# A hybrid decoder layer: the first quarter's input scale computed on TensorE, and the second quarter's embedding moved behind the first head

## The chip, the core and the metric

The kernel runs on one core of a Trainium2 chip. A core has five engines that work side by side, each through its own list of instructions in order: TensorE (PE, matrix products), VectorE (DVE), ScalarE (ACT), GpSimd (POOL) and SyncE (SP), which here only issues transfers. Transfers (DMA) run on the core's 16 DMA engines between device memory and the on-chip buffers. Matrix products accumulate in PSUM, which this kernel uses as eight banks of 128 x 512 fp32 values.

The metric is the device time of one execution in microseconds (us). The median of three runs of the kernel before is 2885.75 us, the lowest 2883.01 and the highest 2885.87.

## The reference, cut to what matters

One decoder layer over T = 2048 tokens with D = 1024 channels, all in fp32. Beside x there is an input p with 256 channels per token.

```python
hn   = rms_norm(x, pre_mix_norm)          # x * rsqrt(mean(x*x) + 1e-6) * w, per token
proj = hn @ w_in                          # q, k, v, z of 4 delta-rule heads; f, i, q, g of 4 HGRN heads; a, b
o_a  = gated delta rule on silu(conv(q, k, v)), decays from a, b, in chunks   # a triangular solve per chunk
o_b  = HGRN2 recurrence from f, i, q
h    = x + rms_norm(concat(o_a * silu(z), o_b * silu(g)) @ w_out, post_mix_norm)
y    = square(relu(rms_norm(h, pre_mlp_norm) @ w_mlp_up)) @ w_mlp_down
h    = h + rms_norm(y, post_mlp_norm)
e    = rms_norm(p @ w_ple_proj, ple_norm) # the embedding: 256 -> 1024 channels
out  = h + e * sigmoid(h @ w_ple_gate)
```

Two results matter here. The scale of x, one rsqrt(mean(x*x) + eps) for each token, is needed before any in-projection can start. The embedding e = p @ w_ple_proj with the sum of its squares is needed only at the very end of the layer.

## The kernel before

**Tiling.** Tokens are worked in four quarters of 512 (`QT`). Activations lie transposed: 128 channels on the partitions, 512 tokens along the row, so that x of a quarter is eight tiles of 128 x 512. Each fp32 operand is split in two float32r halves (`split`, L159 to L162): ACT writes the rounded value (L161), DVE the remainder (L162). A product of two operands is three matmuls (high by high, high by low, low by high), 128 x 128 by 128 x 512 each. A weight of the in-projection is 1024 x 128: it is loaded to a `raw` buffer (two of them, 512 KB), split into a `whl` buffer (three of them), and takes part in 24 matmuls.

**The front** (L329 to L374). PE computes the embedding of quarters 0 and 1, eight tiles each, six matmuls a tile (`embed_tile`, L292, `project`, L190). ACT copies each tile to a buffer `e` (six of them) for a store to device memory (`ed`), and squares it; DVE adds the squares (`squares`, L217). The embedding weight comes in two loads of four tiles (`stage_ple`, L277). For the scale, 2 MB of x are loaded by rows, tokens on the partitions (L338); ACT squares each 1024-wide row with an accumulated sum (L355), POOL raises the four sums per partition to the power -0.5 (`rsqrt`, L156). The result, 128 x 4, is written to device memory (`spread`, L228) and read back as a row that is broadcast to all partitions (`spread_load`, L234). Between the later embedding tiles each of the eight transposed tiles of x is scaled by it and by the norm's weight (`operand`, L197, the scaling L203) and split: these are the in-projection's operands `xt`. `vectors` (L130 to L146) makes the small per-channel constants from the transposed vectors.

**The mixers** (L377 to L935). `works` (L792 to L802) lists the in-projections in order: for each quarter the decays' `ab`, then for each of four heads eight projections (k, q, v, z of the delta rule, f, i, q, g of HGRN). Each is 24 matmuls, done in three steps of eight; after each step `tick()` (L324) runs the parts of other generators that the agenda has at that step. So the written program places, by step number: the delta-rule mixer (`gdn_mixer`, with offsets `A_STEPS` from the head's first projection), the HGRN mixer (`B_STEPS`), the decays (`decays`, L427, ending in the transposes `ps_gb`, L450), the norms of the embedding (`norm_steps`, L255: a split of the sum, two matmuls with ones, a row by way of device memory), the next quarter's scale (`x_scale`, L399, from step 30 of the quarter) and its operands (`load_x`, L820), and the sums of MLP weights (`down_sums`, L859). In quarter 0 `stage_work` loads the weight three works ahead, `split_work` splits it two works ahead, and `keep_work` stores the split weight, which later quarters reload.

**The first head's solve.** `gdn_mixer` sends the four diagonal blocks of its triangular systems through device memory (`ud`, L582 to L589), solves them on DVE in 31 dependent pairs of multiply and reduce (L595, L596, four rows to a step), stores the result (`xd`, L600), loads it back as diagonal blocks (`xx`, L606), transposes (L610), and goes on with the matmuls `psp` (L618).

**What sets the order.** PE's order is the written one throughout (`manual_schedule`, L301). SP's order, and so the order of DMA issues, is written in the front and in the mixers' loop (L331, L889). The orders of DVE, ACT and POOL are chosen by a planner that sorts the instructions of the whole program. Buffers of a pool (`bufs`) make a writer wait for the last reader of the same buffer.

## Time and profile before

| what | value |
|---|---|
| runs, median (lowest to highest) | 2885.75 us (2883.01 to 2885.87) |
| profiled execution, its own time | 2882.39 us |
| span of the profiled execution | 2880.6 us |
| mean granted TensorE clock | 0.988 of full speed |
| PE busy, share of the span | 2780.4 us, 97% |
| DVE busy | 2155.5 us, 75% |
| ACT busy | 1332.7 us, 46% |
| POOL busy | 132.8 us, 5% |
| moved by DMA | 589.71 MB, 205 GB/s in the mean |

The span is that of the instructions; the execution's own time includes what lies around them, 1.8 us here. Rows of the trace that follow give, in order of time: start in us from the span's start, duration in us, engine, line of the kernel, instruction, output and inputs by the program's names, shapes, and how many were grouped ("x24": from the first start to the last end). In brackets stands how long the engine had waited before it and what released it. SPq is SP's queue issuing a DMA. In the page's groups, "A <- B: 12.3, 1, 12.3" is a wait of PE for B ahead of A: sum, count, mean. In the table of stretches each row is one stretch: its bounds, its length, then busy time and number of instructions of PE, weight loads (PEld), DVE, ACT and POOL, then the granted clock of TensorE, the busy share of the DMA engines, and GB/s.

### The profile page before, as it was taken

How to read it: one execution, taken by the hardware profiler on the slowest of the kernel's cores; microseconds unless marked ns; L12 is line 12 of the kernel's file. 1: busy time of each engine (PE TensorE's matmuls, PEld its weight loads, DVE VectorE, ACT ScalarE, POOL GpSimd, SP SyncE). 2: the span in 40 equal slices, each digit the busy share in tenths (PEclk: the TensorE clock that was granted, in tenths of full speed). 3: DMA queues.
4: the chain of work that ended last, by engine and by line, in shares of the span. 5: the costliest groups of instructions: out<-in, count | busy, mean ns of one | idle time of the engine just before them, and what ended most of it. 6: DMA issues, size and time to landing. Idle time of an engine off the chain costs nothing.

```text
span 2880.6 us, 39562 instructions
## 1 busy us (share of the span) xinstructions
PE 2780.4 (97%) x13361; PEld 2296.8 (80%) x13361; DVE 2155.5 (75%) x4700; ACT 1332.7 (46%) x2460; POOL 132.8 (5%) x116
## 2 busy tenths in 40 slices
PE   7899999999999999889999999999999999999999
PEld 5688788888888888767778887888888888887887
DVE  6788788887878787747879987776787765567675
ACT  6444333333324333447556555554555445465431
POOL 0000000000000000120000000000100000001000
PEclk9899999999999999999999999999999999999999
DMA  7666667656655666577746646666664446677563
GB/s 253 228 215 204 221 208 245 204 189 222 220 192 177 209 201 201 177 240 236 250 134 217 235 161 221 221 209 196 210 202 146 157 150 210 188 257 240 194 230 118
DMA packets 268603, 589.71 MB, mean 205 GB/s; under 512 B 55642, under 2 KB 59960, under 8 KB 249072
## 3 DMA queue, kind: packets, MB, share of 16 engines
q1 hardware_dynamic: 268400, 587.18, 61.2%
q8 instruction: 106, 1.74, 0.3%
...
## 4 chain that ended last, share of the span: by engine, by line
PE 47%; DMA 4%; DVE 4%; ACT 2%; issue 2%; POOL 1%; SPq 1%; DVEq 0%; ACTq 0%; POOLq 0%
PE u L953 21%; PE d L953 18%; PE mmg L953 6%; DMA mixT<-mixd 1%; PE mmo L953 1%; DMA da<-sumd 1%; DMA rsb_g<-rd_g 0%; DMA b<-h1d 0%; DMA xo<-in_xT_dram 0%; DMA raw_out<-in_w_out_dram 0%; PE mme L188 0%; DMA dr<-in_w_down_dram 0%; POOL acc_y L225 0%; DVE w_out L162 0%; POOL w_out L162 0%
## 5 line engine op out<-in xcount | busy, mean ns | idle before, releaser
L907 PE MATMUL mm<-xt,w 128*128 128x512 f32 x3072 | 791.5, 405 | 1.0 <-ACT hist L478 1.0
L907 PEld LDWEIGHTS mm<-xt,w 128*128 128x128 f32 x3072 | 564.8, 191 | 120.7 <-ACT hist L478 1.7
L953 PE MATMUL u<-t,wu 128*128 128x512 f32 x2688 | 627.3, 395 | 6.3 <-ACT wu L161 5.2
L953 PE MATMUL d<-db,da 128*128 128x512 f32 x2688 | 612.8, 390 | 4.0 <-ACT db L214 2.0
L953 PEld LDWEIGHTS u<-t,wu 128*128 128x128 f32 x2688 | 507.0, 189 | 125.8 <-ACT wu L161 6.7
L953 PEld LDWEIGHTS d<-db,da 128*128 128x128 f32 x2688 | 504.1, 188 | 112.0 <-DVE db L215 4.4
L215 DVE TENSOR_TENSOR db<-db 128x512 fp32r<-128x512 f32 x224 | 160.6, 717 | 76.0 <-ACT db L214 75.4
L1273 DVE TENSOR_TENSOR u<-u,u 128x512 f32<-128x512 f32 x224 | 150.4, 683 | 68.5 <-PE u L953 68.5
L953 PE MATMUL mmo<-mixT,w_out 128*128 128x512 f32 x768 | 186.7, 404 | 13.4 <-DVE w_out L162 6.3
L953 PEld LDWEIGHTS mmo<-mixT,w_out 128*128 128x128 f32 x768 | 148.2, 194 | 50.7 <-DVE w_out L162 8.0
L214 ACT ACTIVATE db<-db 128x512 fp32r<-128x512 f32 x224 | 140.9, 629 | 87.5 <-DMA db<-hid 82.9
L953 PE MATMUL mmg<-h2T,wg 128*128 128x512 f32 x768 | 177.5, 393 | 0.0
L953 PEld LDWEIGHTS mmg<-h2T,wg 128*128 128x128 f32 x768 | 144.3, 188 | 32.8
L595 DVE TENSOR_TENSOR pr_g<-xs_g,sys_g 128x4 f32<-128x4 f32 (+30 forms) x496 | 138.7, 280 | 32.9 <-DMA sys_g<-ud_g 22.8
L1313 ACT ACTIVATE u<-u 128x512 f32<-128x512 f32 x128 | 80.9, 632 | 170.5 <-DVE u L1273 170.2
L162 DVE TENSOR_TENSOR da<-da 128x512 fp32r<-128x512 f32 x128 | 93.8, 733 | 85.8 <-ACT da L161 85.2
L161 ACT ACTIVATE da<-da 128x512 fp32r<-128x512 f32 x128 | 80.5, 629 | 130.6 <-DMA da<-sumd 114.1
L596 DVE TENSOR_REDUCE xs_g<-pr_g 128x4 f32<-128x8 f32 (+30 forms) x496 | 111.0, 224 | 9.9
L161 ACT ACTIVATE wu<-a 128x512 fp32r<-128x512 f32 x128 | 76.4, 622 | 56.4 <-DMA a<-in_w_up_dram 54.4
L225 POOL TENSOR_TENSOR acc_y<-acc_y,sq_y 128x512 f32<-128x512 f32 x28 | 38.6, 1379 | 1379.1 <-ACT sq_y L224 1379.1
L162 DVE TENSOR_TENSOR wu<-a,wu 128x512 fp32r<-128x512 f32 x128 | 87.5, 687 | 8.5 <-ACT wu L161 8.2
L706 PE MATMUL at_h<-q_h,k_h 128*128 128x64 f32 x640 | 82.7, 273 | 2.1 <-DVE tail_g L528 1.4
(355 smaller groups left out, 3839.9 us busy)
## 6 DMA issues: line engine op xcount, KB each, us to landing
...
db<-hid SPq DMA_DIRECT2D x224, 256.0 KB
...
a<-in_w_up_dram SPq DMA_DIRECT2D x128, 256.0 KB
hid<-u SPq DMA_DIRECT2D x128, 256.0 KB
da<-sumd SPq DMA_DIRECT2D x128, 256.0 KB
...
```

What stands on the lines that cost most here:

```text
L161: S.activation(t[:, 0], raw, AF.Copy)
L162: eng.tensor_tensor(t[:, 1], raw, t[:, 0], ALU.subtract)
L214: S.activation(t[:, 0], plain(t), AF.Copy)
L215: V.tensor_tensor(t[:, 1], plain(t), t[:, 0], ALU.subtract)
L225: eng.tensor_tensor(acc, acc, sq, ALU.add)
L595: V.tensor_tensor(pr[:, :, 0:i], xs[:, :, 0:i], sys[:, None, 0:i, i].broadcast_to([P, GC, i]), ALU.mult)
L596: V.tensor_reduce(xs[:, :, i], pr[:, :, 0 : i + 1], AX.X, ALU.add)
L706: PE.matmul(ps[:, c, :], k[:, blk(c)], odd, start=True, stop=True)
L907: PE.matmul(ps, *terms[i], start=i == 0, stop=i == nt - 1)
L953: PE.matmul(ps, a, b, start=start, stop=stop)
L1273: V.tensor_tensor(c[new], c[old], ps, ALU.add)
L1313: S.activation(c[k], c[k], AF.Relu)
```

## The change

1. *The scale of the first x.* The loads of x by rows are gone. The eight transposed tiles of x, loaded anyway, are squared by ACT, two at a time (four operations of 128 x 1024), and added by DVE to one 128 x 512 tile. Four matmuls with one column of ones sum it over the partitions, with 128 tokens on the partitions of each column. After scaling, POOL's power gives the 128 x 4 values; DVE multiplies the identity by them (`diag`), and one fp32 matmul of ones by `diag` gives the scale of every token on all partitions, in a PSUM bank that DVE reads directly when it scales the tiles.
2. *The front's order.* SP, ACT and DVE follow the written order there (`first`), not the planner's. The embedding's eight tiles of quarter 0 go to banks of two pools (`homes`); their squares are kept in four pairs (`esq`) and summed after the operands. `vectors` is split in two: the transposed columns early, the rest after the operands. The weights of `ab` and of the first projection (`4_0_0`) are staged in the front.
3. *The second quarter's embedding* leaves the front. It becomes two works (`plee0`, `plee1`) of 24 matmuls each behind the first head's eight projections of quarter 0, four tiles a work. Its input p is loaded and split from step 16 (`load_p`); each tile is copied to one of two buffers of the pool `m2` and its store is issued at once (`leave`).
4. *What follows from it.* Quarters start at the steps in `qstart`. The second quarter's `x_scale` starts at step 40 rather than 30. The norm of the first embedding runs at steps 2 to 7, that of the second after `plee1`.

The diff, cut to its core (`stage` is moved out of the mixers with its text unchanged; `leave` is the second half of `embed_tile`):

```diff
-    def vectors():
-
+    def columns_of_rows():
         ps = bank("ps_rows", pp)
         PE.transpose(ps[:, :N_ROWS], rows, ident[:N_ROWS, :N_ROWS])
         V.tensor_copy(cols, ps[:, :N_ROWS])
+
+    def vectors():
...
-        def ready(eng):
+        def ready(eng, then=None):
             w = wp.tile([P, 2, KD, P], F32R, tag="whl", name=f"w_{name}")
             for half in range(2):
                 sl = slice(half * KD // 2, (half + 1) * KD // 2)
                 split(w[:, :, sl], eng, raw[:, sl])
+                if half == 0 and then is not None:
+                    then()
+            return w
+
+        return ready
+
+    def stage(name, src, k=KD):
...
+        return leave(ps, q, d, accs, pool, bufs)
+
+    def leave(ps, q, d, accs, pool, bufs):
...
-        with tc.manual_schedule(engines={mybir.EngineType.SP}):
+        first = {mybir.EngineType.SP, mybir.EngineType.Activation, mybir.EngineType.DVE}
+        with tc.manual_schedule(engines=first):
             ple0 = stage_ple(0, "plea0")
-            praw = [es.tile([P, 2, QT], F32, name=f"praw{q}") for q in range(2)]
-            nc.sync.dma_start(praw[0], pT[:, tok(0)].rearrange("(k p) t -> p k t", p=P))
-            rows4 = x[tok(0), :].rearrange("(p c) d -> p c d", c=NC)
-            xs = es.tile([P, NC, D], F32, name="xs")
-            for c in range(0, NC, 2):
-                nc.sync.dma_start(xs[:, c : c + 2], rows4[:, c : c + 2])
+            praw = es.tile([P, 2, QT], F32, name="praw0")
+            nc.sync.dma_start(praw, pT[:, tok(0)].rearrange("(k p) t -> p k t", p=P))
             nc.sync.dma_start(ident, consts[:, C_IDENT])
             nc.sync.dma_start(rows, vecs)
-            nc.sync.dma_start(dec[:, 0:1], gdn_a_log.rearrange("o h -> h o"))
-            nc.sync.dma_start(dec[:, 1:2], gdn_dt_bias.rearrange("o h -> h o"))
-            nc.sync.dma_start(praw[1], pT[:, tok(1)].rearrange("(k p) t -> p k t", p=P))
-            ple1 = stage_ple(1, "plea1")
             xraw = es.tile([P, KD, QT], F32, name="xraw")
             for k in range(0, KD, 2):
                 nc.sync.dma_start(xraw[:, k : k + 2],
                                   xT[k * P : (k + 2) * P, tok(0)].rearrange("(k p) t -> p k t", p=P))
+            nc.sync.dma_start(dec[:, 0:1], gdn_a_log.rearrange("o h -> h o"))
+            nc.sync.dma_start(dec[:, 1:2], gdn_dt_bias.rearrange("o h -> h o"))
+            ple1 = stage_ple(1, "plea1")
+            ab_ready, w0_ready = stage("ab0", w_ab), stage("4_0_0", w_in[4])
             nc.sync.dma_start(cst[:, C_NEG:], consts[:, C_NEG:])
 
-            ple = [ple0(V), None]
-            pts = [[operand(ra, None, f"pT{q}_{k}", raw=praw[q][:, k]) for k in range(2)] for q in range(1)]
+            pt, ple, es_sq, stores = [], {}, {}, []
+            ple[0] = ple0(V, lambda: pt.extend(operand(ra, None, f"pT0_{k}", raw=praw[:, k]) for k in range(2)))
+            p1 = [ra.tile([P, 2, QT], F32R, tag="ring", name=f"pT1_{k}") for k in range(2)]
+            homes = (pm, pm, pp, pp, pp, pp, pm, pm)
+            sums = {}
+
+            def embed(d):
+                sums[d] = bank(f"mme_0_{d}", homes[d])
+                project(sums[d], ple[d // 4][:, :, 2 * (d % 4) : 2 * (d % 4) + 2], pt)
+
+            def put(d):
+                if d % 2 == 0:
+                    es_sq[d // 2] = es.tile([P, 2, QT], F32, name=f"esq{d // 2}")
+                e = es.tile([P, QT], F32, tag="ld", name=f"e0_{d}", bufs=KD)
+                S.activation(e, sums[d], AF.Copy)
+                S.activation(es_sq[d // 2][:, d % 2], sums.pop(d), AF.Square)
+                nc.sync.dma_start(ed[0][d], e)
+
+            total = es.tile([P, 2, QT], F32, name="xtotal")
+
+            def x_squares(k):
+                if k == 0:
+                    S.activation(total, xraw[:, :2], AF.Square)
+                else:
+                    sq = es.tile([P, 2, QT], F32, tag="xsq", name=f"xsq{k}", bufs=2)
+                    S.activation(sq, xraw[:, k : k + 2], AF.Square)
+                    V.tensor_tensor(total, total, sq, ALU.add)
+
+            embed(0)
+            columns_of_rows()
+            x_squares(0)
+            embed(1)
+            put(0)
+            x_squares(2)
+            embed(2)
+            x_squares(4)
+            put(1)
+            embed(3)
+            x_squares(6)
+            acc = st.tile([P, QT], F32, tag="acc", name="acc_x0", bufs=3)
+            V.tensor_tensor(acc, total[:, 0], total[:, 1], ALU.add)
+
+            ps = bank("ss_x0", po)
+            for c in range(NC):
+                PE.matmul(ps[:, c : c + 1], acc[:, blk(c)], one[:, 0:1], start=True, stop=True)
+            ple[1] = ple1(V)
             ss = sm.tile([P, NC], F32, tag="ss", name="ss_x0")
-            for c in range(NC):
-                S.activation(xs[:, c], xs[:, c], AF.Square, accum_out=ss[:, c : c + 1])
-            V.tensor_scalar(ss, ss, 1.0 / D, EPS, ALU.mult, ALU.add)
+            V.tensor_scalar(ss, ps[:, :NC], 1.0 / D, EPS, ALU.mult, ALU.add)
             rsqrt(ss)
-            stores = []
-            for d in range(4):
-                stores.append(embed_tile(0, d, ple[0], pts[0], accs, es, 6))
-                if d == 1:
-                    vectors()
-            pts.append([operand(ra, None, f"pT1_{k}", raw=praw[1][:, k]) for k in range(2)])
-            ple[1] = ple1(V)
-            x_r[0] = spread(ss, "x0")
-            rsb = spread_load(x_r[0], "x0")
-            for d, q in [(d, 1) for d in range(4)] + [(d, q) for d in range(4, KD) for q in range(2)]:
-                stores.append(embed_tile(q, d, ple[d // 4], pts[q], accs, es, 6))
-                stores.pop(0)()
-                if len(xts[0]) < KD:
-                    k = len(xts[0])
-                    xts[0].append(operand(ra, None, f"xt0_{k}", col(R_PREMIX + k), rsb, raw=xraw[:, k]))
-            for f in stores:
-                f()
+            put(2)
+            split_w = {0: ab_ready()}
+            diag = es.tile([P, NC, P], F32, name="xdiag")
+            V.tensor_tensor(diag, over_chunks(ident), ss[:, :, None].broadcast_to([P, NC, P]), ALU.mult)
+            rsb = bank("rs_x0", po)
+            PE.matmul(rsb, one, diag.rearrange("p c n -> p (c n)"), start=True, stop=True)
+            put(3)
+            for d in range(4, KD):
+                embed(d)
+            for k in range(KD):
+                xts[0].append(operand(ra, None, f"xt0_{k}", col(R_PREMIX + k), rsb, raw=xraw[:, k]))
+                if k % 2:
+                    put(4 + k // 2)
+            vectors()
+            pair = es_sq[0]
+            for i in range(1, KD // 2):
+                V.tensor_tensor(pair, pair, es_sq[i], ALU.add)
+            accs[0] = st.tile([P, QT], F32, tag="acc", name="acc_e0", bufs=3)
+            V.tensor_tensor(accs[0], pair[:, 0], pair[:, 1], ALU.add)
...
+        qstart = []
         for q in range(NQ):
+            qstart.append(SPT * len(works))
             works.append((f"ab{q}", "ab", w_ab, q, None, None, None, None))
...
+                if (q, h) == (0, 0):
+                    works += [(f"plee{i}", None, i, 0, None, None, None, None) for i in range(2)]
         last = t + LAST
-        staged, split_w = {}, {}
+        staged = {1: w0_ready}
 
...
-                staged[j] = stage(works[j][0], works[j][2])
+                name, key, src = works[j][:3]
+                staged[j] = stage(name, src) if key else partial(stage_ple(src, name), V)
...
-            if works[j][3] == 0:
+            if works[j][3] == 0 and works[j][1]:
                 keep(works[j][1], split_w[j])
+
+        def load_p():
+
+            raws = [m2.tile([P, QT], F32, tag="ld", name=f"raw_pT1_{k}", bufs=2) for k in range(2)]
+            for k in range(2):
+                nc.sync.dma_start(raws[k], pT[blk(k), tok(1)])
+            yield
+            for k in range(2):
+                split(p1[k], V, raws[k])
 
...
-        per_q = SPT * (1 + 8 * 4)
-        starts = [per_q * q + 5 + n * i for q, m, n in ((1, 6, 14), (2, 5, 16), (3, 5, 16)) for i in range(m)]
+        starts = [qstart[q] + 5 + n * i for q, m, n in ((1, 6, 14), (2, 5, 16), (3, 5, 16)) for i in range(m)]
         for g, t in enumerate(starts):
             at(t, down_sums(g), (0, 4, 6, 10))
         for q in range(1, NQ):
-            at(per_q * (q - 1) + 30, x_scale(q), range(0, 20, 2))
-            at(per_q * q, load_x(q), range(-9, 0))
-            call(per_q * q, boundary)
-        for q in range(2):
-            at(0, norm_steps(accs[q], 1.0 / D, EPS, f"e{q}", partial(ple_r.__setitem__, q)),
-               [4 * q + i for i in (0, 2, 4, 5)])
+            at(qstart[q - 1] + (40 if q == 1 else 30), x_scale(q), range(0, 20, 2))
+            at(qstart[q], load_x(q), range(-9, 0))
+            call(qstart[q], boundary)
+        at(0, norm_steps(accs[0], 1.0 / D, EPS, "e0", partial(ple_r.__setitem__, 0)), (2, 4, 6, 7))
+        at(16, load_p(), (0, 3))
         with tc.manual_schedule(engines={mybir.EngineType.SP}):
-            stage_work(0)
-            stage_work(1)
-            split_work(0)
             stage_work(2)
             split_work(1)
             for j, (name, key, src, q, h, then, g, b) in enumerate(works):
                 split_work(j + 2)
                 stage_work(j + 3)
                 keep_work(j)
+                if key is None:
+                    w = split_w.pop(j)
+                    for s in range(SPT):
+                        for i in range(s * 24 // SPT, (s + 1) * 24 // SPT):
+                            k, term = i % 6 // 3, i % 3
+                            if i % 6 == 0:
+                                ps = bank(f"mme_1_{4 * src + i // 6}")
+                            PE.matmul(ps, w[:, term // 2, 2 * (i // 6) + k, :], p1[k][:, term % 2, :],
+                                      start=i % 6 == 0, stop=i % 6 == 5)
+                            if i % 6 == 5:
+                                leave(ps, 1, 4 * src + i // 6, accs, m2, 2)()
+                        tick()
+                    if src == 1:
+                        at(clock[0], norm_steps(accs[1], 1.0 / D, EPS, "e1", partial(ple_r.__setitem__, 1)),
+                           (1, 3, 5, 6))
+                    continue
                 ps = bank(f"mm_{name}")
                 w, xt = split_w.pop(j), xts[q]
                 terms = []
```

15 lines of the change are left out of this document (6 added, 9 removed).

## The prediction

> **What bounds the kernel now.** I read the page's engine shares first, then a table of stretches of the first 140 us, then what TensorE (PE) waited for there, then its instructions in order of time.
>
> ```profile
> PE 2780.4 (97%) x13361; PEld 2296.8 (80%) x13361; DVE 2155.5 (75%) x4700; ACT 1332.7 (46%) x2460; POOL 132.8 (5%) x116
> ...
> 20.00:30.00 10.00, 4.43 (x19) 3.04 (x17) 5.04 (x8) 5.62 (x10) 0.00 (x0) 0.95 0.96 338
> 120.00:140.00 20.00, 8.72 (x34) 7.66 (x35) 10.73 (x31) 4.41 (x12) 0.00 (x0) 0.57 0.51 171
> ...
> PE psp_g L618 <- DVE xx_g L610: 12.3, 1, 12.3
> ```
>
> PE is busy for 97% of the span, so time is won or lost only where PE stands. In the first 140 us it does so in two places: the front, before the first in-projection matmul (20 to 30 us: 4.43 of 10 busy), and once in the first head, 12.3 us ahead of `psp`, the matmuls that wait for VectorE's (DVE's) triangular solve of that head.
>
> ```profile
> 46.47 5.87 PE L907 MATMUL mm_ab<-xt,w_ab 128*128 128x512 f32 x24 [0.30 <-ACT sq_e L224]
> 52.18 0.40 PE L261 MATMUL nrm_e<-hl_e,ones 128*128 128x512 f32 x1
> ...
> 61.35 1.19 PE L450 MATMUL ps_gb<-cst,gb 36*128 36x36 f32 x4 [0.61 <-DVE gb L442]
> ...
> 83.18 18.91 PE L907 MATMUL mm<-xt,w 128*128 128x512 f32 x80
> ...
> 131.28 2.04 PE L618 MATMUL psp_g<-xx_g,um 128*128 128x128 f32 x8 [12.29 <-DVE xx_g L610]
> ...
> 134.68 3.72 PE L907 MATMUL mm<-xt,w 128*128 128x512 f32 x8
> 138.23 0.60 PE L486 MATMUL t_kg<-cst,y_kg 128*128 128x128 f32 x4
> ...
> 146.94 1.05 PE L618 MATMUL psp_g<-xx_g,um 128*128 128x128 f32 x8
> ```
>
> The reader is to see three marks: in-projection from 46.47, decay transposes `ps_gb` at 61.35, `psp` at 131.28. A warm matmul of 512 columns costs 18.91/80 = 0.236 us. After the stall PE is slow: the 6.95 us from 131.28 to 138.23 hold 8 `psp` (2.04 here, 1.05 at 146.94), 8 `at_h` of like length and 8 matmuls (3.72 here, 1.9 at 0.236 each); at full pace, with their overlaps, that is about 3.7, so the cold restart costs 3.3.
>
> **How the change is to be counted.** Up to `psp` PE passes as many matmuls after the change as before: 34 steps of 8. Before, all 272 belong to the in-projection; after, 48 of them are the second quarter's embedding, taken from the front, and 48 in-projection matmuls are left for later: 48 x 0.236 = 11.3 us. So
>
> difference = (move of `psp`'s start) + 11.3 - (cold restart saved, at most 3.3).
>
> The change breaks even only if `psp` starts 8.0 us earlier, at 123.3. What follows asks when it starts.
>
> **The front: the scale.** These rows price it.
>
> ```profile
> 0.74 0.44 SPq L280 DMA_DIRECT2D raw_plea<-in_w_ple_dram  x1
> 4.85 1.15 ACT L161 ACTIVATE w_plea<-raw_plea 128x512 fp32r<-128x512 f32 x2 [2.84 <-DMA raw_plea<-in_w_ple_dram]
> 7.30 5.32 PE L188 MATMUL mme<-pT,w_plea 128*128 128x512 f32 x12 [7.30 <-ACT pT L161]
> 9.15 1.06 ACT L355 ACTIVATE xs<-xs 128x1024 f32<-128x1024 f32 x1 [1.39 <-DMA xs<-in_x_dram]
> 11.24 0.58 ACT L297 ACTIVATE e<-mme 128x512 f32<-128x512 f32 x1
> 11.72 0.58 ACT L221 ACTIVATE acc_e<-mme 128x512 f32<-128x512 f32 x1
> 17.11 0.38 SPq L418 DMA_DIRECT2D raw_ab<-in_w_ab_dram  x1
> 19.32 0.68 DVE L162 TENSOR_TENSOR w_plea<-raw_plea,w_plea 128x512 fp32r<-128x512 f32 x1
> 25.03 1.06 ACT L161 ACTIVATE w_ab<-raw_ab 128x1024 fp32r<-128x1024 f32 x1 [2.32 <-DMA raw_ab<-in_w_ab_dram]
> 28.08 2.08 DVE L203 SCALAR_TENSOR_TENSOR xraw<-xraw,cols,rsb_x 128x512 f32<-128x512 f32 x3 [0.73 <-DMA rsb_x<-rd_x]
> 33.26 0.63 ACT L161 ACTIVATE xt<-xraw 128x512 fp32r<-128x512 f32 x1 [0.67 <-DVE xraw L203]
> 40.60 1.22 DVE L162 TENSOR_TENSOR w<-raw,w 128x1024 fp32r<-128x1024 f32 x1
> ```
>
> Gone are the two 1 MB loads of x by rows, their squares, and the scale's trip through DRAM that released DVE at 28.08. In their place the first embedding tile ends near 10.2 (its six cold matmuls at 0.44, from 5.32/12, and one wait for a split). ScalarE (ACT) then does, in the written order, two pairs of 512-wide operations (pitch 0.48) and three 1024-wide squares (0.96 to 1.06): 10.25 + 2 x 0.98 + 3 x 1.0 = 15.2. The 2 MB of transposed x that it squares take the place, in the load queue, of 2 MB of rows whose first half was in use at 9.15, so I add no wait for them. DVE adds the last square (1.22), folds (0.69), splits the second embedding weight (2 x 0.64): 18.4. The four one-column matmuls, POOL's power, the diagonal and the matmul with ones, which the trace does not show together, follow from the fold at 17.1.
>
> But DVE's first scaled tile stands behind the split of `4_0_0`'s weight, whose load can be issued only when the second embedding weight has left its buffer, at 18.4. A 512 KB load takes 4.1 us on an empty queue (0.74 to 4.85) and 7.9 behind others (17.11 to 25.03); the queue is nearly empty here, so 4.1: 22.5, ACT 1.06, DVE 1.22, thus 24.85. The short operations of the scale have 7.7 us until then, and cost nothing unless they take more. Scaling starts 3.2 us earlier than the 28.08 of before.
>
> **The front: the eight operands.** Written by hand, DVE takes scale, waits for ACT's half, takes its own half, and only then the next tile: 0.75 + 0.63 + 0.62 and two hand-overs of 0.03 to 0.04, 2.07 us each, 16.6 for eight, and 0.5 where a 1024-wide split falls in between: 41.9. PE's first projection follows tile by tile and ends near 42.2, against 52.3: a lead of 10 us.
>
> **Where the lead goes.** Behind the last operand DVE still has a queue, and PE's first norm, now 16 matmuls into the next projection, waits for its end.
>
> ```profile
> 52.31 1.03 DVE L392 MEMSET um<- 128x512 f32 x2
> 53.31 1.15 DVE L396 MEMSET S<- 128x128 f32 x8
> ...
> 53.01 0.57 ACT L264 ACTIVATE acc_e<-nrm_e 1x512 f32<-1x512 f32 x1
> 53.49 1.04 ACT L161 ACTIVATE w<-raw 128x1024 fp32r<-128x1024 f32 x1
> ...
> 57.63 0.63 ACT L438 ACTIVATE se<-se 4x512 f32<-4x512 f32 x1
> ```
>
> The small vectors (ten operations, five dependent, about 1.6), three dependent 1024-wide adds that replace the embedding's running sum (3 x 1.22), a weight split (1.15), a fold (0.65), the memsets (2.3), the norm's split (0.65): 41.7 + 10.0 = 51.7. Before, the norm ran at 52.18. PE, which could be there at 46, stands about 5.5 us. Behind the norm on ACT come its row, the decays' tanh, exp, table load and logarithm: before, 53.01 to 58.26, of which 1.6 are a weight split and a second norm's split that are not there now; so 52.6 + 3.65 = 56.25, 2.0 earlier. DVE's scan and `ps_gb` follow at 59.35. Of 10 us of lead 2.0 are left. From here to the solve PE had waited about 1 us in all before, so the lead stays 2.0.
>
> **The solve.**
>
> ```profile
> 96.80 0.17 DVE L595 TENSOR_TENSOR pr_g<-xs_g,sys_g 128x4 f32<-128x4 f32 x1 [2.83 <-DMA sys_g<-ud_g]
> ...
> 111.33 0.32 DVE L595 TENSOR_TENSOR pr_g<-xs_g,sys_g 128x84 f32<-128x84 f32 x1
> ...
> 111.96 0.32 DVE L595 TENSOR_TENSOR pr_g<-xs_g,sys_g 128x88 f32<-128x88 f32 x1
> ...
> 112.83 0.75 DVE L476 SCALAR_TENSOR_TENSOR acc_kg<-mm,cols,acc_kg 128x509 f32<-128x509 f32 x1
> ...
> 125.68 0.28 DVE L596 TENSOR_REDUCE xs_g<-pr_g 128x4 f32<-128x128 f32 x1
> ...
> 125.99 0.32 SPq L600 DMA_DIRECT2D xd_g<-xs_g  x1
> ```
>
> Its input load now stands behind two 256 KB loads of p: +0.5 (their bytes mostly fit the wait for `ud`). Start 96.8 - 2.0 + 0.5 = 95.3. It took 29.2 us. Out of it go the second head's convolutions for k and q (six at pitch 0.66 and two closing products, 5.3), the first attention masks (1.5), four weight splits (4.6); in come four half splits of the embedding weights (2.5), two weight splits (2.3), two sums of squares (1.2): -5.4. Bare steps cost 0.63 (111.33 to 111.96) against some 0.45 with work between: +1.3. So 25.1 us, end 120.4, against 126.0.
>
> **The embedding behind the first head.** Its 48 matmuls would fill PE's stall, but each tile is copied to one of two buffers and stored. In the changed order of SyncE's queue the solve's own store `xd` stands ahead of the second tile's store: SP waits there until 120.4. The fourth tile's copy needs that buffer, ACT is behind it, and PE's sixth tile needs the bank: from about 117 PE stands.
>
> ```profile
> 45.95 1.65 SPq L299 DMA_DIRECT2D ed<-e  x2
> ...
> 52.16 0.09 DVE L389 MEMSET bound<- 128x36 f32 x1 [1.85 <-DMA ed<-e]
> ...
> 127.53 0.17 DVE L593 COPY xs_g<-cst 128x4 f32<-128x4 f32 x1 [1.30 <-DMA xd_g<-xs_g]
> ...
> 111.75 0.59 PE L691 MATMUL at_h_d<-att_h,one 128*128 128x256 f32 x2
> 112.18 1.05 PE L694 MATMUL at_h<-hb_h,k_h 128*128 128x128 f32 x8
> ```
>
> A 64 KB store was seen done 1.54 us after its issue (125.99 to 127.53), a 256 KB one behind 1 MB 4.9 us (47.28, the last issue of that row, to 52.16). The queue is idle, so 1.54 and 0.65 for the bytes: 2.2. Store at 120.8, done 123.0, copy and square 1.1, PE on at 124.15: six cold matmuls (0.43 each), the masks' matmuls (1.24, cold 2.5), two tiles of 1.4, eight matmuls 1.9: `psp` at 134.0. The four `xx` loads end earlier and hide. Move of `psp`: +2.7.
>
> The Trainium skill, page "DMA: Bandwidth & Descriptors", section "Latency and other measured facts", puts the fixed cost of a DMA at about 2 us, mostly the receipt. By it, an estimate, the store takes 2.65 and the sum is 0.4 larger; the 1.54 us row says less than 2.
>
> **Costed at nothing.** Two more embedding weight loads and their splits (counted in the solve); the second quarter's squares, ten steps later (needed some 40 steps on); the second embedding's norm (its result is used after the MLP). If that cover went, each is under 2 us.
>
> **Sum.** 2.7 + 11.3 - 3.3 = +10.7 us on 2882.4 for the profiled execution: 2893.1. The median of the runs is 2885.75, 3.4 above the profiled one; the forecast for the median is 2896.5.
>
> **Rivals.**
> 1. Not slower: the front's lead reaches the solve whole. It decides at DVE's queue between 41.7 and 51.7: if that ran beside the projection, `ps_gb` would come 10.1 earlier instead of 2.0, `psp` at 125.9: -5.4 + 11.3 - 3.3 = +2.6, 2888.4. For it: the single items are cheap; against it: DVE runs in order and none of them is behind the split. Break-even at a lead of 12.7. Were the stores free as well, `psp` would start 5.3 behind the solve, at 117.6: -5.7, 2880.
> 2. The stores do not hold PE: then `psp` waits only for `xx`, 5.3 us behind the solve, at 125.7: -5.6 + 11.3 and no cold cost saved: +5.7, 2891.5. It decides if the second store is issued before the solve ends.
> 3. Upper bounds: the weight's load 7.9 instead of 4.1 and the store 4.9 instead of 2.2: +6.5, 2903.
>
> That the embedding is not moved, or the order not kept, is excluded by the order of the changed program, engine by engine.
>
> **How the numbers follow.** My sum 0.58 (2892 to 2901); rival 1 0.11, with free stores a further 0.10; rival 2 0.12; rival 3 0.09. A measurement here can tell about 0.2%, 5.8 us. Slower: 0.58 + 0.09 + half of rival 2 = 0.73. Faster: 0.10 and 0.02 of rival 1 = 0.12. Same: the rest, 0.15. The range leaves out the faster case and a little at the top: 2887 to 2904.
>
> **What would show it.** In the changed profile: first scaled tile near 25, `mm_ab` spread to 42; PE waiting some 5 us for `hl_e` near 52; `ps_gb` near 59; solve from 95 to 120; PE idle from 117 until a square of an embedding tile near 124; `psp` near 134; from there the same work, 11 us more of it. The prediction is wrong if `psp` starts before 126, or if the waits later in the first quarter, which I left as they are, change by more than 4 us.

## The result and the profile after

The median of the runs after is 2903.68 us (2900.3 to 2906.92), beside 2884.38 for the kernel before on the same chip: a ratio of 1.0064, 95% interval 1.0052 to 1.0077. The change costs 0.64%, some 18.5 us. The forecast was +10.7 us and a median of 2896.5; the time lies in the forecast range of 2887 to 2904, at its very top. The profiled execution, the fastest of the four, took 2900.3 us with a span of 2898.5, 17.9 more than before.

First the engine shares, from the page of the kernel after.

```profile
PE 2786.2 (96%) x13371; PEld 2301.8 (79%) x13371; DVE 2165.5 (75%) x4706; ACT 1334.7 (46%) x2460; POOL 133.1 (5%) x116
```

PE has 5.8 us more busy time and ten more instructions, against 17.9 us of span: 12.1 of these are PE standing. Where it stands is told by the waits of PE in the kernel after, over the whole execution (sum, count, longest).

```profile
PE psp_g L666 <- DVE xx_g L658: 12.9, 4, 6.1
PE mme L963 <- ACT sq_e L226: 10.8, 2, 6.0
...
PE mm_ab L980 <- ACT esq L382: 7.4, 1, 7.4
```

The 12.3 us ahead of the first `psp` have gone from the list. In their place stand two waits of the moved embedding for a PSUM bank that ACT has yet to free (10.8), one of `mm_ab` (7.4), and a 6.1 us wait of a `psp` that is not the first head's; the other three of `psp`, 6.7 us together, lie in later quarters, and the kernel before has 6.9 us there. PE's instructions of the kernel after, in order of time, place them:

```profile
37.52 8.30 PE L980 MATMUL mm_ab<-xt,w_ab 128*128 128x512 f32 x24 [7.39 <-ACT esq L382]
...
51.80 0.50 PE L264 MATMUL nrm_e<-hl_e,ones 128*128 128x512 f32 x1 [1.75 <-DVE hl_e L164]
...
59.05 1.26 PE L498 MATMUL ps_gb<-cst,gb 36*128 36x36 f32 x4 [3.02 <-DVE gb L490]
...
116.38 2.93 PE L963 MATMUL mme<-pT,w_plee 128*128 128x512 f32 x6 [4.84 <-ACT sq_e L226]
...
125.28 1.22 PE L963 MATMUL mme<-pT,w_plee 128*128 128x512 f32 x2 [5.97 <-ACT sq_e L226]
...
135.79 1.05 PE L666 MATMUL psp_g<-xx_g,um 128*128 128x128 f32 x8
...
221.85 2.05 PE L666 MATMUL psp_g<-xx_g,um 128*128 128x128 f32 x8 [6.14 <-DVE xx_g L658]
...
228.11 0.60 PE L534 MATMUL t_kg<-cst,y_kg 128*128 128x128 f32 x4
...
346.33 2.12 PE L980 MATMUL mm_ab<-xt,w_ab 128*128 128x512 f32 x8
```

The same three later marks in the kernel before:

```profile
201.73 1.05 PE L618 MATMUL psp_g<-xx_g,um 128*128 128x128 f32 x8
...
205.38 0.60 PE L486 MATMUL t_kg<-cst,y_kg 128*128 128x128 f32 x4
...
328.87 2.12 PE L907 MATMUL mm_ab<-xt,w_ab 128*128 128x512 f32 x8
```

The reader can follow the lag from mark to mark: -2.3 us at `ps_gb` (59.05 against 61.35), +4.5 at the first `psp` (135.79 against 131.28), +20.1 at the second head's (221.85 against 201.73, of which 11.3 are the 48 matmuls that have changed places), and +17.5 where the second quarter begins (346.33 against 328.87). All but 0.4 us of the difference of 17.9 is made in the first quarter. The second head's `psp` did not wait before; now it waits 6.14 us.

### The profile page after: what moved, and what is told of

The parts are those of the page before. It is cut to its first block, busy times and chain, and to the rows that moved or that the text cites. A ratio compares the mean times of both kernels' runs of the same rounds, so it can differ in the third digit from the quotient of the medians.

```text
span 2898.5 us, 39573 instructions
## 1 busy us (share of the span) xinstructions
PE 2786.2 (96%) x13371; PEld 2301.8 (79%) x13371; DVE 2165.5 (75%) x4706; ACT 1334.7 (46%) x2460; POOL 133.1 (5%) x116
## 4 chain that ended last, share of the span: by engine, by line
PE 46%; DMA 4%; DVE 4%; ACT 2%; issue 2%; POOL 1%; SPq 1%; DVEq 0%; ACTq 0%; POOLq 0%
PE u L1026 21%; PE d L1026 18%; PE mmg L1026 6%; DMA mixT<-mixd 1%; DMA da<-sumd 1%; PE mmo L1026 0%; DMA xo<-in_xT_dram 0%; DMA rsb_g<-rd_g 0%; DMA raw_out<-in_w_out_dram 0%; POOL w_out L164 0%; DMA b<-h1d 0%; DVE w_out L164 0%; DVE t L164 0%; PE mme L190 0%; ACT L1063 0%
## 5 line engine op out<-in xcount | busy, mean ns | idle before, releaser
L644 DVE TENSOR_REDUCE xs_g<-pr_g 128x4 f32<-128x8 f32 (+30 forms) x496 | 111.5, 225 | 10.3
L227 POOL TENSOR_TENSOR acc_y<-acc_y,sq_y 128x512 f32<-128x512 f32 x28 | 38.7, 1381 | 1377.1 <-ACT sq_y L226 1377.1
```

The source lines that it names most:

```text
L227: eng.tensor_tensor(acc, acc, sq, ALU.add)
L644: V.tensor_reduce(xs[:, :, i], pr[:, :, 0 : i + 1], AX.X, ALU.add)
```

## The experiments

The forecast's theory was that DVE's and ACT's written order eats the front's lead, and that stores in SyncE's queue hold the embedding. The 6.14 us of the second head were in no part of it. The experiments e1 to e8 each take one part of this by itself; c1 to c4 combine edits. All are edits of the kernel after, unless another is named. The marks are the starts of `ps_gb` and of the first `psp`, and PE's wait ahead of the second head's `psp`; they are those of one execution each.

| kernel | ratio to before | 95% interval | `ps_gb` | `psp` | wait, second head |
|---|---|---|---|---|---|
| after | 1.0064 | 1.0052 to 1.0077 | 59.05 | 135.79 | 6.14 |
| e1_place_only | 1.0010 | 0.9997 to 1.0022 | 52.44 | 126.43 | 4.48 |
| e2_scale_only | 1.0035 | 1.0024 to 1.0047 | 68.44 | 145.69 | 0 |
| e3_xd_later | 1.0058 | 1.0039 to 1.0076 | 59.97 | 134.18 | 5.44 |
| e4_finish_later | 1.0040 | 1.0028 to 1.0052 | 58.47 | 138.46 | 1.30 |
| e5_planner | 1.0024 | 1.0013 to 1.0035 | 48.88 | 129.09 | 5.47 |
| e6_pipe | 1.0039 | 1.0023 to 1.0054 | 56.29 | 130.70 | 5.42 |
| e7_tail | 1.0032 | 1.0020 to 1.0045 | 59.93 | 133.15 | 5.59 |
| e8_act_store | 1.0043 | 1.0028 to 1.0059 | 59.77 | 131.35 | 5.61 |
| c1_place_fin_act | 0.9972 | 0.9961 to 0.9983 | 52.16 | 116.12 | 2.14 |
| c2_plan_fin_act | 0.9997 | 0.9986 to 1.0008 | 48.81 | 122.42 | 1.58 |
| c3_late | 0.9979 | 0.9969 to 0.9988 | 51.69 | 118.25 | 1.67 |
| c4_ud_early | 0.9973 | 0.9964 to 0.9983 | 48.79 | 117.57 | 2.65 |

Below, a gain against the kernel after is the difference of two ratios of this table; its interval adds the two half widths as squares, some 0.2% throughout, so that gains of 0.21 to 0.25% are just clear of it. The marks scatter too: e4 has, up to the first `psp`, the same instructions in the same order on DVE, ACT and POOL as the kernel after, and yet its solve starts 2.7 us later (99.40; 96.70, each time behind a wait for the load of `sys`) and its `psp` 2.67 later. Smaller differences of `psp` are not told apart here.

### Each half of the change alone

e1 keeps the old scale and the old order of the front and only moves the second quarter's embedding (the early staging of two weights goes too, and the first norm runs at steps 0, 2, 4 and 5). In the diffs the minus side is the kernel after.

```diff
-        first = {mybir.EngineType.SP, mybir.EngineType.Activation, mybir.EngineType.DVE}
-        with tc.manual_schedule(engines=first):
+        with tc.manual_schedule(engines={mybir.EngineType.SP}):
...
+                nc.sync.dma_start(xs[:, c : c + 2], rows4[:, c : c + 2])
...
+                S.activation(xs[:, c], xs[:, c], AF.Square, accum_out=ss[:, c : c + 1])
...
-            PE.matmul(rsb, one, diag.rearrange("p c n -> p (c n)"), start=True, stop=True)
...
+            x_r[0] = spread(ss, "x0")
+            rsb = spread_load(x_r[0], "x0")
             for d in range(4, KD):
-                embed(d)
...
+                stores.append(embed_tile(0, d, ple[1], pts, accs, es, 6))
+                stores.pop(0)()
+                for k in (2 * (d - 4), 2 * (d - 4) + 1):
+                    xts[0].append(operand(ra, None, f"xt0_{k}", col(R_PREMIX + k), rsb, raw=xraw[:, k]))
...
```

> Only the second part of the change: the front is that of before (x loaded by rows, the planner's order, without the second quarter's tiles), and the second quarter's embedding stands behind the first head, at two buffers, as in the changed kernel. Theory (the place carries the loss): the front loses the embedding's cover and gains little, the stall behind the second tile's store and the one at the second head's psp are as in the changed kernel, and the time is 14 to 22 us above before. Rival (the new front carries it: cold TensorE, 23.9 us idle up to ps_gb against 17.3): this kernel is at most 11 us above before.

e2 keeps the new scale and the new order of the front, and leaves the second quarter's embedding in the front, its squares added on GpSimd:

```diff
...
+                ps1 = bank(f"mme_1_{k}", pp)
+                project(ps1, ple[k // 4][:, :, 2 * (k % 4) : 2 * (k % 4) + 2], p1)
                 xts[0].append(operand(ra, None, f"xt0_{k}", col(R_PREMIX + k), rsb, raw=xraw[:, k]))
...
+                leave(ps1, 1, k, accs, es, KD, eng=G)()
...
-                if (q, h) == (0, 0):
-                    works += [(f"plee{i}", None, i, 0, None, None, None, None) for i in range(2)]
...
-            at(qstart[q - 1] + (40 if q == 1 else 30), x_scale(q), range(0, 20, 2))
+            at(qstart[q - 1] + 30, x_scale(q), range(0, 20, 2))
-        at(16, load_p(), (0, 3))
```

> Only the first part of the change: the scale by small matmuls and the written order of the front, but the second quarter's embedding stays in the front, on TensorE between the first quarter's tiles and the in-projection (its squares are added on GpSimd, and its norm runs at steps 8 to 13); the next quarter's scale starts at step 30 again. Theory: operands are ready near 42 us with TensorE busy meanwhile, ps_gb comes 1 to 4 us earlier than 61.35, the first head's stall stays, and the time is 0 to 5 us below before. Rival (the new front carries the loss): 6 us or more above before.

PE's `ps_gb` in e1:

```profile
52.44 0.43 PE L456 MATMUL ps_gb<-cst,gb 36*128 36x36 f32 x4
```

and `psp` in e2:

```profile
145.69 2.05 PE L672 MATMUL psp_g<-xx_g,um 128*128 128x128 f32 x8 [12.76 <-DVE xx_g L664]
```

The new place alone is not measurably slower (+0.10%, its interval holds zero), so the theory's +14 to +22 us for it fell. With the old scale and its trip through device memory `ps_gb` comes 6.6 us earlier than with the new scale in its written order (52.44 against 59.05): it isn't the embedding that costs most, it is the front. e2 says the same from the other side: `ps_gb` 7.1 us later than before, the 12.76 us stall where it was, +0.35%, the rival's side of its forecast. It is the weaker of the two, since more work stands in the written order there than in either kernel. And in e1 the second head still waits 4.48, so that wait belongs to the embedding's place; in e2 it is 0.

### The front: who writes the order

e5 gives DVE's and ACT's order in the front back to the planner:

```diff
-        first = {mybir.EngineType.SP, mybir.EngineType.Activation, mybir.EngineType.DVE}
+        first = {mybir.EngineType.SP}
```

> The changed kernel with one edit: in the front only SyncE's order is the written one; VectorE's and ScalarE's are the planner's again, as in the kernel before. The scale by small matmuls and the embedding behind the first head stay. Theory (the written order of the front costs more than the new scale brings): VectorE scales tiles ahead of ScalarE's halves and has the small vectors behind it before the operands, the last operand is ready near 37 us instead of 41.3, ps_gb comes at 51 to 54 instead of 59.05, psp at 125 to 129, and the time is 6 to 14 us below the changed kernel. Rival (the scale by small matmuls itself is what the front lost): ps_gb at 58 or later, time within 2 us of the changed kernel.

DVE's instructions of the kernel after and then of e5:

```profile
24.34 0.74 DVE L205 SCALAR_TENSOR_TENSOR xraw<-xraw,cols,rs_x 128x512 f32<-128x512 f32 x1
...
40.62 0.69 DVE L164 TENSOR_TENSOR xt<-xraw,xt 128x512 fp32r<-128x512 f32 x1 [0.70 <-ACT xt L163]
```

```profile
24.47 2.06 DVE L205 SCALAR_TENSOR_TENSOR xraw<-xraw,cols,rs_x 128x512 f32<-128x512 f32 x3
...
34.48 1.30 DVE L164 TENSOR_TENSOR xt<-xraw,xt 128x512 fp32r<-128x512 f32 x2
...
40.93 0.63 DVE L164 TENSOR_TENSOR hl_e<-acc_e,hl_e 128x512 fp32r<-128x512 f32 x1
```

PE's `ps_gb` of e5:

```profile
48.88 1.26 PE L498 MATMUL ps_gb<-cst,gb 36*128 36x36 f32 x4 [3.03 <-DVE gb L490]
```

Scaling starts at the same time in both (24.34 and 24.47), but the planner runs three scalings in a row, so that DVE need not wait for ACT's half within a tile: the eighth operand ends at 35.8 instead of 41.3, and the norm's split at 41.6, where in the kernel after the norm stands at 51.80. `ps_gb` gains 10.2 us, `psp` 6.7, the time 0.40% (some 11.5 us). The theory held, and `ps_gb` came 2 us earlier than it said. Of the 10.2 us 5.5 are the operands; the other 4.7 are DVE's queue behind them, since from the last operand to the norm it is 5.8 us (35.8 to 41.6) instead of 10.5 (41.3 to 51.8).

e6 leaves the order written and only scales one tile ahead:

```diff
...
+                if k + 1 < KD:
+                    scale_x(k + 1)
-                xts[0].append(operand(ra, None, f"xt0_{k}", col(R_PREMIX + k), rsb, raw=xraw[:, k]))
+                t = ra.tile([P, 2, QT], F32R, tag="ring", name=f"xt0_{k}")
+                split(t, V, xraw[:, k])
...
```

> The changed kernel, its written order kept, with one edit: VectorE scales tile k+1 before it takes its half of tile k, so that it no longer waits for ScalarE in each tile (eight tiles at about 1.3 us instead of 2.05). Theory A (the serial operands cost): the last operand near 36.5, mm_ab ends 4 us earlier, ps_gb near 55, time 3 to 6 us below the changed kernel. Theory B (VectorE's tail behind the operands decides, whatever their pitch): ps_gb stays within 1.5 us of 59.05.

One tile ahead is worth 0.25% (some 7 us): the last operand is ready at 36.1 instead of 41.3, `ps_gb` comes 2.8 earlier and `psp` 5.1. So the hand-over between DVE and ACT inside each tile is a good part of what e5 won, as theory A had it.

e7 leaves the operands as they are and clears DVE's queue behind them: `vectors` goes ahead of the operands, the sum of the squares and the memsets go to POOL, the norm is asked for later.

```diff
             put(0)
+            vectors()
...
-                V.tensor_tensor(pair, pair, es_sq[i], ALU.add)
+                G.tensor_tensor(pair, pair, es_sq[i], ALU.add)
...
-            V.memset(t, 0.0)
+            G.memset(t, 0.0)
...
-        at(0, norm_steps(accs[0], ...), (2, 4, 6, 7))
+        at(0, norm_steps(accs[0], ...), (10, 12, 14, 15))
```

> The changed kernel, the operands serial as they are, with VectorE's tail taken away: the small vectors stand right behind the first tile's copies, the sum of the embedding's squares and the clearing of um, S and bound run on GpSimd, and the first embedding's norm runs at steps 10, 12, 14 and 15 instead of 2, 4, 6 and 7. Theory B (the tail decides): TensorE's waits of 1.75 and 3.02 us ahead of the norm and of ps_gb go, ps_gb comes at 51 to 54, time 5 to 9 us below the changed kernel. Theory A (the serial operands decide): ps_gb no earlier than 57.

The edit brought waits of its own. ACT, GpSimd and VectorE in the trace of e7, in order of time:

```profile
13.58 0.20 ACT L147 ACTIVATE nexpa<-dec 4x1 f32<-4x1 f32 x1 [2.18 <-DMA dec<-in_gdn_a_log_dram]
...
23.68 2.34 POOL L432 TENSOR_TENSOR esq<-esq,esq 128x1024 f32<-128x1024 f32 x1
23.74 2.83 DVE L420 TENSOR_TENSOR xdiag<-cst,ss_x 128x512 f32<-128x512 f32 x1 [0.92 <-POOL ss_x L159]
```

ACT waits 2.18 us for the decays' vector ahead of the squares, the diagonal takes 2.83 us instead of 0.69 beside a POOL add, and the scale is ready 5.4 us later (26.63; 21.26 in the kernel after). `ps_gb` therefore stays at 59.93, where theory A had it, but not for theory A's reason. From the end of `mm_ab` (52.5; 45.8) to `ps_gb` it takes 7.5 us instead of 13.2, and the time is 0.32% better (some 9 us), as theory B had it. That DVE's queue behind the operands also holds the path is what e5's 4.7 us show; e7 fits it, but doesn't show it alone, since it moves the norm as well and its `psp` is only 2.6 us earlier.

### The embedding's stores and the solve's

e3 asks for the solve's store `xd` four steps later, its loads `xx` three and their transposes two, so that `xd` is queued behind the embedding's stores:

```diff
+                if (q, h) == (0, 0):
+                    a_steps = A_STEPS[:14] + (28, 29, 30, 30) + A_STEPS[18:]
```

> The changed kernel with one edit: the first head's store of the solve (xd), its loads xx and its transposes are issued 4, 3 and 2 steps later in the written order, so that the stores of the first six embedding tiles stand ahead of xd in SyncE's queue. psp stays where it is on TensorE. Theory (the store behind xd holds TensorE): the wait of 5.97 us ahead of the sixth tile goes, psp starts at 128 to 131 instead of 135.79, and the time falls by 4 to 7 us. Rival (psp is bound by the solve's end and the idle time only moves): psp moves by less than 1.5 us, and so does the time.

e8 leaves the order and issues the embedding's stores on ACT's queue:

```diff
-        return lambda: nc.sync.dma_start(ed[q][d], e)
+        return lambda: queue.dma_start(ed[q][d], e)
...
-                                leave(ps, 1, 4 * src + i // 6, accs, m2, 2)()
+                                leave(ps, 1, 4 * src + i // 6, accs, m2, 2, nc.scalar)()
```

> The changed kernel with one edit: the second quarter's embedding tiles are stored from ScalarE's queue, behind the copy that ScalarE makes, instead of SyncE's, so that none stands behind the solve's store xd. Theory (that queue holds TensorE): the wait of 5.97 us ahead of the sixth tile goes, xx is issued some 2 us earlier (three stores no longer ahead of it), psp starts at 128 to 131 instead of 135.79, time 4 to 7 us below the changed kernel. Rival (the wait of 4.84 us ahead of the fifth tile, ScalarE's copies standing behind weight splits that wait for a load, and the solve's end decide): psp moves by less than 2 us.

SyncE's issues in the kernel after, and the solve's last step on DVE:

```profile
83.44 0.33 SPq L299 DMA_DIRECT2D raw<-in_w_in_dram  x1
...
84.72 3.53 SPq L633 DMA_DIRECT2D ud_g<-u_g  x4
...
121.31 0.29 DVE L644 TENSOR_REDUCE xs_g<-pr_g 128x4 f32<-128x128 f32 x1
...
121.63 0.33 SPq L648 DMA_DIRECT2D xd_g<-xs_g  x1
122.07 3.01 SPq L318 DMA_DIRECT2D ed<-e  x3
...
209.49 0.32 SPq L648 DMA_DIRECT2D xd_g<-xs_g  x1
...
213.85 0.32 SPq L276 DMA_DIRECT2D rd_g<-m_g  x1
...
215.23 1.80 SPq L654 DMA_DIRECT2D xx_g<-xd_g  x4
```

in e3:

```profile
123.29 3.14 SPq L318 DMA_DIRECT2D ed<-e  x2
...
127.61 0.28 DVE L644 TENSOR_REDUCE xs_g<-pr_g 128x4 f32<-128x128 f32 x1
...
127.92 0.32 SPq L648 DMA_DIRECT2D xd_g<-xs_g  x1
```

and the solve's last step and PE's `psp` in e8:

```profile
125.66 0.28 DVE L644 TENSOR_REDUCE xs_g<-pr_g 128x4 f32<-128x128 f32 x1
...
131.35 1.13 PE L666 MATMUL psp_g<-xx_g,um 128*128 128x128 f32 x8 [2.79 <-DVE xx_g L658]
```

In the kernel after the embedding's next stores leave from 122.07 on, right behind `xd` at 121.63, which waited for the solve's end at 121.60; the issue before it was at 110.97. The queue was blocked at its head. The Trainium skill, page "DMA: Bandwidth & Descriptors", section "Anatomy of one DMA — SWDGE (gpsimd) path", says that a wait for a semaphore is spent on the issuing sequencer and not in the DMA engines; these rows agree, since for 10 us SyncE issued nothing that stood behind `xd`.

Both experiments take PE's 5.97 us wait away (in e8 1.30 us are left of it), and both then meet the solve. In e3 `xd` is issued at 127.92, but the stores now ahead of it don't hold it: the last of them was issued by 126.43, and the solve itself ends only at 127.89. It started at 99.41, 2.7 us later than in the kernel after, which is within the scatter, and it lasted 28.5 us instead of 24.9: PE, no longer held, gives DVE the attention masks (L744 to L760) and more of the embedding's sums (L227) while the solve runs, and DVE works them between its steps. `psp` gains 1.6 us, and the time cannot be told from that of the kernel after (1.0058 and 1.0064), which is nearly the rival's case. In e8 the solve lasts 28.3 us for the same reason and ends at 125.94. But now `xx` leaves 1.57 us behind `xd` (125.96 and 127.53) instead of 3.55, and `psp` comes 5.4 us behind the solve's end instead of 14.2: it is 4.4 us earlier, and the time 0.21% (some 6 us) better. So the stores cost 8.8 us between solve and `psp`; of what their removal gives, 3.4 are taken back by a longer solve, and 1.0 is a later start of it.

### The second head

The same listing shows the new 6.14 us wait. `xd` of the second head is issued at 209.49; its `xx` loads, which need only its arrival (in e8's first head they left 1.57 us behind it), only at 215.23. Between them stands `rd_g` at 213.85, the closing norm of the first head, which waits for POOL and DVE. The first two heads begin 30 steps apart instead of 24, since two works of three steps stand between them. `xx`, at offset 26 of the second head, thus moves from step 50 to step 56 of the first, and the first head's `rd_g`, at its step 55, now comes ahead of it. e4 asks for that finish later:

```diff
+                if (q, h) == (0, 0):
+                    a_steps = A_STEPS[:-3] + (58, 60, 62)
```

> The changed kernel with one edit: the last three parts of the first head's closing norm (its store rd, its scale and the store of its result) run at offsets 58, 60 and 62 instead of 55, 57 and 59, so that the second head's loads xx no longer stand behind that store in SyncE's queue. Theory (the queue holds the second head's xx, issued at 215.23 although xd was issued at 209.49): xx is issued 3 to 4 us earlier, TensorE's wait of 6.14 us ahead of the second head's psp falls to about 2, and the time falls by 3 to 6 us. Rival (the second solve itself ends too late, at 209.4, VectorE having more other work in it): the wait stays above 5 us and the time within 1 us.

SyncE's issues in e4, and behind them PE's `psp`:

```profile
212.19 0.32 SPq L648 DMA_DIRECT2D xd_g<-xs_g  x1
...
215.46 1.75 SPq L654 DMA_DIRECT2D xx_g<-xd_g  x4
...
219.78 1.13 PE L666 MATMUL psp_g<-xx_g,um 128*128 128x128 f32 x8 [1.30 <-DVE xx_g L658]
```

From `xd` to `xx` it is now 3.27 us instead of 5.74, and the wait is 1.30 instead of 6.14. Of these 4.84 us about 2 are an earlier `psp`, and 2.8 come from PE, which arrives later (218.48; 215.71), as it was already 2.67 us later at the first head's, ahead of anything the edit moves. `psp` runs warm (1.13 instead of 2.05). The time is 0.24% (some 7 us) better (the theory: 3 to 6).

### Together

Here e1's and e5's fronts are joined with the edits of e4 and e8. c1 is e1 with these two; c2 is e5 with them.

```diff
 # c1: e1_place_only     c2: e5_planner     both:
+                if (q, h) == (0, 0):
+                    a_steps = A_STEPS[:-3] + (58, 60, 62)
-                                leave(ps, 1, 4 * src + i // 6, accs, m2, 2)()
+                                leave(ps, 1, 4 * src + i // 6, accs, m2, 2, nc.scalar)()
```

> The front of before without the second quarter's tiles (e1_place_only), with the two later mends together: the first head's closing norm 3 steps later (e4_finish_later) and the embedding tiles stored from ScalarE's queue (e8_act_store). Theory (three separate losses: the written front, the store behind xd, the second head's xx behind rd): each mend keeps its own gain, some 6 us and some 4 us on the 2887.4 of that run's span, so a span near 2877 and a time 3 to 8 us below before. Rival (the gains overlap, and the next chain, the first head's solve, takes them back): not below before.

> The changed kernel with three edits: the planner's order for VectorE and ScalarE in the front (e5_planner), the first head's closing norm 3 steps later (e4_finish_later), the embedding tiles stored from ScalarE's queue (e8_act_store). It keeps the scale by small matmuls. Theory: from the 2890.7 of the planner's run some 10 us go, a span near 2880 and a time within 4 us of before. If the scale by small matmuls is worth anything once the written order is gone, this kernel is faster than c1_place_fin_act; by the two profiles so far (solve started at 89.69 with it, 87.09 without) it is 1 to 4 us slower.

c1 beats the kernel before by 0.28% (interval 0.17% to 0.39%). c2 has the earlier front (`ps_gb` 48.81 against c1's 52.16), yet its first `psp` is 6.3 us later and its time only that of the kernel before. (The execution profiled of c2 is the slowest of its twelve, 2890.89 us against a median of 2882.51.) The gain of 3.3 us is lost between the two marks, and the trace of c2 says where (DVE and SyncE in order of time):

```profile
68.76 0.60 DVE L619 SCALAR_TENSOR_TENSOR u_g<-kk_g,ncc_g,e_g 128x128 f32<-128x128 f32 x2
...
72.78 1.23 DVE L164 TENSOR_TENSOR w<-raw,w 128x1024 fp32r<-128x1024 f32 x1 [2.48 <-ACT w L163]
...
74.03 0.33 SPq L299 DMA_DIRECT2D raw<-in_w_in_dram  x1
...
75.69 1.55 SPq L633 DMA_DIRECT2D ud_g<-u_g  x2
...
89.79 0.17 DVE L643 TENSOR_TENSOR pr_g<-xs_g,sys_g 128x4 f32<-128x4 f32 x1 [4.62 <-DMA sys_g<-ud_g]
```

The solve's input u is complete at 69.36, but its store `ud` stands in SyncE's queue behind a weight load that can only be issued when a DVE split has freed its buffer, at 74.01. So `ud` leaves 6.3 us late, and the solve starts at 89.79 instead of c1's 85.24. The kernel after has the same order: there the load leaves at 83.44 and `ud` at 84.72.

c3 asks, in c1, for the first norm and for p later. c4 asks, in c2, for `ud` one step earlier, ahead of that load:

```diff
 # c3, on c1
-        at(0, norm_steps(accs[0], ...), (0, 2, 4, 5))
-        at(16, load_p(), (0, 3))
+        at(0, norm_steps(accs[0], ...), (10, 12, 14, 15))
+        at(18, load_p(), (0, 3))
 # c4, on c2
-                    a_steps = A_STEPS[:-3] + (58, 60, 62)
+                    a_steps = A_STEPS[:5] + (11,) + A_STEPS[6:-3] + (58, 60, 62)
```

> c1_place_fin_act with two more edits: the first embedding's norm runs at steps 10, 12, 14 and 15 instead of 0, 2, 4 and 5, and the loads of the second quarter's p are issued at step 18, behind the solve's input load sys, instead of between it and its source. Theory (what the front and the loads of p hold reaches the first head's psp, since TensorE waits there): the 2.87 us wait ahead of the norm goes, the solve starts 2 to 4 us earlier than in c1, and the time is 2 to 4 us below c1. Rival (both lie beside TensorE's other work): within 1.5 us of c1.

> c2_plan_fin_act with one edit: the first head's stores ud (and the transposes of v) run at offset 11 instead of 12, which puts ud ahead of a weight load in SyncE's queue that waits for a split on VectorE. In c2 the source u was ready at 69.4 and ud was issued at 75.69. Theory (SyncE's queue takes the lead of the new scale before it reaches the solve): ud is issued near 70.5, the solve starts 3 to 5 us earlier than c2's 89.79, psp comes 2 to 4 us earlier than 122.42, and the time is 2 to 5 us below c2. Rival (the load sys itself, among the weight traffic, sets the solve's start): the solve starts within 1.5 us of 89.79.

c3 changes nothing that can be told from c1 (0.9979 and 0.9972), as its rival had it. In c4 one number in a list of steps moves the solve by 4.6 us; SyncE and DVE in its trace:

```profile
68.39 1.87 SPq L633 DMA_DIRECT2D ud_g<-u_g  x4
...
85.20 0.17 DVE L643 TENSOR_TENSOR pr_g<-xs_g,sys_g 128x4 f32<-128x4 f32 x1 [0.74 <-DMA sys_g<-ud_g]
```

`psp` is 4.85 us earlier than in c2, the time 0.24% better, a little more than the theory said, and c4 is 0.27% faster than the kernel before (interval 0.17% to 0.36%). c4 still holds both halves of the change, the scale by matmuls and the embedding behind the first head. So what made the change slower is the order of the queues, DVE's and ACT's in the front and SyncE's, with the step offsets that feed it. Two things stay open. c1, with the old scale, and c4, with the new one, cannot be told apart, so no run shows a gain of the scale by matmuls. And the kernel before has a late `ud` too (u complete at 81.78, `ud` issued at 85.44); what an earlier one is worth there was not run, so c4's lead need not be the change's alone. At the start of the second quarter c4's profiled execution is only 2.0 us ahead of that of before (326.89 against 328.87), at the start of the fourth 5.6 (890.84 against 896.42); what wins there, and the rest up to its 9.2 us of span, was not traced.

## Why the prediction was right in sign and short in size

**The front, right.** Its first scaled tile came at 24.34 (forecast 24.85), the operands' pitch was 2.05 us and the last ended at 41.3 (41.9), the norm ran at 51.80 (51.7) and `ps_gb` at 59.05 (59.35): a lead of 2.3 us left out of ten, as forecast. (The sum for the norm starts at 41.7, 0.2 us ahead of its own end of the operands; this changes nothing.) That the hand-overs within the operands and the queue behind them eat it is shown by e5 (5.5 and 4.7 us), the hand-overs alone by e6. One number inside was wrong: `mm_ab` was to end near 42.2 and ended at 45.8. It had to wait for its bank, which ACT freed only by squaring the embedding's seventh tile at 37.47, and then ran cold; the stretch of 30 to 40 us of the kernel after (bounds, length, busy time of PE, its loads, DVE, ACT and POOL, then granted clock, DMA share, GB/s):

```profile
30.00:40.00 10.00, 2.60 (x7) 2.00 (x7) 7.76 (x11) 5.55 (x10) 0.00 (x0) 0.63 0.94 353
```

The granted clock was 0.63 here, 0.50 from 37.5 to 42.0 and 0.88 from there to 45.8, and the 24 matmuls took 8.30 us; before, at a clock of 1.00, it was 5.87. By the rows this cost nothing, because the norm at 51.80 waited for DVE, as forecast; PE stood only 1.75 us ahead of it, not some 5.

**The solve, right.** Two more rows of DVE in the kernel after:

```profile
96.70 0.17 DVE L643 TENSOR_TENSOR pr_g<-xs_g,sys_g 128x4 f32<-128x4 f32 x1 [2.66 <-DMA sys_g<-ud_g]
...
123.18 0.17 DVE L641 COPY xs_g<-cst 128x4 f32<-128x4 f32 x1 [1.32 <-DMA xd_g<-xs_g]
```

It starts at 96.70, 1.4 later than the forecast 95.3: the extra sits in `ud`, queued behind the weight load above. It lasts 24.9 us (25.1 forecast), and ends at 121.6 (120.4), where `xd` is issued. PE goes on at 125.28 (124.15), and `psp` at 135.79 (134.0): a move of 4.5 us where 2.7 was forecast. A second wait of 4.84 us, from 111.5 to 116.4, was not forecast: ACT stood behind two weight splits that waited for transfers. It is likely to have cost nothing, since PE would have stood for the store in any case, but that was not tested. From the solve's end to `psp` it is 14.2 us (13.6 forecast). The store's 1.54 us, taken from a row of before, was 1.55 here (121.63 to 123.18), which is under the figure of about 2 us in the Trainium skill, page "DMA: Bandwidth & Descriptors", section "Latency and other measured facts". The embedding's store took 2.07 us to the copy that waited for it (122.07 to 124.14; 2.2 forecast). That stores held behind the solve's in SyncE's queue hold PE is shown by e8, and by e3, where PE's wait goes as well. The cold restart saved is 3.3 us as forecast: between the first head's two `psp` it is 12.38 us (135.79 to 148.17), before 15.66.

**The rivals.** Rival 1's mechanism is real: where DVE's queue is out of the way `psp` comes at 129.09 (e5) and 126.43 (e1, +0.10%), which the rival had put at 125.9 and +2.6 us. It was not this kernel's case. With free stores as well it is that of c4 and, by the old front, of c1, both faster, as the rival's second part had said (`psp` at 117.6 and -5.7 us; measured 117.57 and 116.12, -0.27% and -0.28%); both also hold e4's edit, without which the second head would have cost them more than the rival counts. Rival 2 was e8's case: `psp` 5.4 us behind the solve's end, where it had 5.3. But it came at 131.35, not at 125.7, since the solve ended at 125.94 instead of 120.4; that a freed PE lengthens the solve was in no part of the forecast. Rival 3 did not come: the weight's load took 3.7 us (issued at 18.37, in use at 22.10) and the store 2.07, where the rival had 7.9 and 4.9.

**The step that fell short.** It is the one that reads "the waits later in the first quarter, which I left as they are", costed at nothing. The prediction itself named a change of more than 4 us there as a sign that it is wrong, and 6.14 us came. The embedding's two works put six more steps between the first two heads, and so moved the first head's last steps ahead of the second head's `xx` in SyncE's queue: 6.1 us of wait, and 2.6 of cold matmuls behind it (from that `psp` to `t_kg` 6.26 us, 3.65 before). e4 takes most of the wait away and 0.24% of the time with it. Some of this came back: the stretch from `t_kg` to the second quarter, before and then after,

```profile
205.38:328.87 123.49, 117.02 (x664) 99.35 (x662) 102.49 (x302) 51.47 (x110) 6.50 (x6) 0.99 0.65 214
```

```profile
228.11:346.33 118.22, 114.72 (x663) 98.45 (x662) 99.36 (x294) 51.40 (x110) 5.41 (x5) 1.00 0.64 218
```

has 3.0 us less idle time of PE (6.47 and 3.50, length less busy). The sum by the forecast's formula with measured terms is 4.5 + 11.3 - 3.3 = 12.5; with 6.1 + 2.6 - 3.0 it is 18.2, against a lag of 17.5 measured. It does not close exactly: between the two `psp` 1.5 us more were lost than these terms say (15.6 against 14.1), and the last stretch has 2.3 us less busy time of PE; what makes these two was not traced.

So of the 7 us by which the forecast fell short, 1.8 are the term "move of `psp`'s start" (4.5 for 2.7, less than the scatter of this mark), and about 5 are the second head, which had no term. That 2903.68 us still lies within 2887 to 2904 is in part luck: the sum's own share of the range ended at 2901, and what reaches to 2904 was there for rival 3's 2903 us, neither of whose conditions came true.
